# A two-layer hybrid encoder: the feed-forward features in other parts, more seven-product pairs in two units, and the first unit's copies dealt out

## The chip, the core and the metric

The kernel runs on one core of a Trainium2 chip. The core has TensorE (PE, the matmul engine; PEld is its weight load), VectorE (DVE), ScalarE (ACT), GpSimd (POOL) and SyncE (SP), which issues most of the transfers. The metric is the device time of one execution in microseconds (us). The kernel before takes 1952.31 us, the median of 3 runs (1952.17 to 1952.49).

## What is computed

One sequence of 256 tokens of width 2048 goes through two residual layers. Layer 0 mixes tokens by attention, layer 1 by a gated recurrence; behind each mixer stands a feed-forward block with 5632 features. All numbers are float32. The part that this change is about is the feed-forward block:

```python
def swiglu(h, w_gate, w_up, w_down):
    return (jax.nn.silu(h @ w_gate) * (h @ w_up)) @ w_down

for i in range(DEPTH):                      # DEPTH = 2
    h = rms_norm(x, norm_mix[i])
    mix = attention_mixer(...) if i % 2 == 0 else recurrent_mixer(...)
    x = x + mix
    x = x + swiglu(rms_norm(x, norm_ffn[i]), w_gate[i], w_up[i], w_down[i])
```

## The kernel before

**Number format.** To keep float32 precision, each operand is split into a rounded part `hi` and a rest `lo`. A product of two blocks of 128 x 128 by 128 x 512 is then three matmuls (`product`, lines 321 to 327): hi by hi, lo by hi, hi by lo. Weights arrive in `raw` tiles of 512 KB through SP's queue. ScalarE casts `raw` to `hi` (line 145, or 163 and 170), and VectorE takes the rest `lo = raw - hi` (line 146, or 164 and 171). Rings of buffers (`landing`, `parts`) let the loads, the casts and the rests run ahead of TensorE by a few tiles.

**Units.** The feed-forward features are worked on in eleven units of four tiles of 128 features (512 features). The units are numbered from 0. For one unit, the 2048 input features are read in eight chunks `c`; each chunk brings one tile of gate weights and one of up weights. There are two ways to multiply a chunk:

- *plain*: two loads (`load_half`), eight products, 24 matmuls. VectorE does two rests of 128 x 1024.
- *a seven-product pair* (`load_seven`, lines 154 to 195): the gate and up blocks are combined in the manner of Strassen so that seven products do, 21 matmuls. VectorE does two rests of 128 x 1024 (line 164), three combinations of 128 x 512 (line 169) and three rests of them (line 171); ScalarE casts accordingly (lines 163 and 170). One more sum, `t1`, is made by an accumulating transfer on POOL's queue (line 176), or by VectorE (line 174) where the three loads in front are all plain.

`SEVEN` names the chunks that are seven-product pairs: 0, 1, 2, 4, 5, 6. `FEWER` names another set for single units: unit 0 has three (0, 5, 6), unit 1 three (4, 5, 6), unit 2 four (1, 4, 5, 6). All other units have six.

**The end of a unit.** When a unit's products are done, VectorE and ScalarE put the four sums together (lines 769 to 773 and 791 to 795), apply SiLU and multiply. VectorE transposes the result in blocks of 32 (line 408), and sixteen small copies (line 416) bring the blocks to their places. A last cast and rest (lines 801 and 802) make the `hi` and `lo` of the features for the down product. With `beside` true, the sixteen copies are not done at once: they are put on the list `tail` in four lots of four, and each following `load_seven` takes one lot (lines 179 and 180), the fourth together with the last cast and rest. Before the change this is so for units 1 to 9; unit 0 and unit 10 do theirs at once, unit 0 with all sixteen on ScalarE.

**Parts.** The down product sums over features, and the sums are made part by part. `PARTS` counts the tiles of the parts: 8, 8, 8, 8 and 12, that is two units each and three in the last. `ffn_plan` (lines 208 to 215) writes out the order of the work. After each unit of part p + 1 come two of the four down groups (512 output columns each) of part p. A group of a part with 8 tiles is 48 matmuls in two accumulators. ScalarE evicts each accumulator to a tile `form` (line 818; two such tiles take turns) and POOL's queue adds it to the residual `x` by an accumulating transfer (line 821). The last part is handled by `groups` (lines 355 to 364): its last unit has just been computed, so two groups first do the tiles that were ready earlier (`front`), then the rest; each finished group is added to `x` by VectorE and, in layer 0, its norm is taken (`Norm.add`); in layer 1 it is stored.

**What sets the order.** TensorE's order is the order of the program. The casts and the rests follow one another in program order (`behind`); the rest of the order on the other engines is set by a scheduler with a timeline. `ahead` and `parted` hold small rules for it: `ahead` lets the n-th rest from now on come after a given instruction; `parted` holds evictions of odd down groups, which the next `load_seven` places behind its casts (lines 191 and 192). The argument `soon` of `unit` chooses earlier places for the end of a unit; it is true for the units of the first part.

Of the kernel before, what the change touches and what calls it, by code (L numbers as in the profile page):

```python
# [24 lines left out]
GROUP = NQ // NKV  # L25
NBLK = 8
DFF = 5632
PARTS = [8, 8, 8, 8, 12]
UNIT = 4
SEVEN = (0, 1, 2, 4, 5, 6)  # L30
FEWER = {0: (0, 5, 6), 1: (4, 5, 6), 2: (1, 4, 5, 6)}
HALF = 8
CHUNK = HALF * P
WIDE = 512
# [40 lines left out]
def trunk(ctx, tc, w, out):  # L75
    nc = tc.nc
    act, dve, pool, pe, sync = nc.scalar, nc.vector, nc.gpsimd, nc.tensor, nc.sync
# [11 lines left out]
    def nm(s):  # L89
        uid[0] += 1  # L90
        return f"{s}_{uid[0]}"

    def tmp(tag, shape=(P, S), dt=F32, bufs=2):
        pl = tp if tag in COMMON else scope[-1]
        return pl.tile(list(shape), dt, tag=tag, name=nm(tag), bufs=bufs)
# [4 lines left out]
    def follow(i, j):  # L100
        tc.add_manual_dep(
            i.ins, j.ins.name,
            mybir.DependencyInfo(mybir.DependencyClass.NoSync, mybir.DependencyReason.DATA),
            reason="order",
        )


    ring, held, ft, ahead, tail, parted = [0], [], [], [], [], []
# [95 lines left out]
    def out_order(src, late=1):  # L204
        groups = [pairs(src[g]) for g in range(NW)]
        return sum([g[:-late] for g in groups[:2]] + [g[-late:] for g in groups[:2]] + groups[2:], [])

    def ffn_plan():
        at = np.cumsum([0] + PARTS) // UNIT
        plan = [("unit", i) for i in range(at[1])]  # L210
        for p in range(len(PARTS) - 1):
            for n, i in enumerate(range(at[p + 1], at[p + 2])):
                plan.append(("unit", i))
                plan += [("down", (p, g)) for g in range(2 * n, min(2 * n + 2, NW))]
        return plan

    def ffn_order(l):
        seq = []
        for what, i in ffn_plan():
# [3 lines left out]
            both = [(w[f"w_gate{l}"][i, c], w[f"w_up{l}"][i, c]) for c in range(KT // 2)]  # L223
            seq += sum(([b] if c in (FEWER.get(i, SEVEN)) else list(b) for c, b in enumerate(both)), [])
        return seq + out_order(w[f"w_down{l}_{len(PARTS) - 1}"], UNIT // 2)

# [11 lines left out]
    def half():  # L238
        n = taken[0]
        taken[0] += 1  # L240
        if n == 0:
            return load_half(order[n], 2, first_x, 2)
        if n < KT // 2 and n % 2 == 0:
            load_x(2 * n, 4)
        if n == KT // 2 - 2:
            load_tables()
        got = load_seven(order[n], all(isinstance(o, bass.AP) for o in order[n - 3 : n])) if isinstance(order[n], tuple) else load_half(order[n], 2 if n == 1 else 1)
        g = n - KT // 2 - 1
        if 0 <= g < NW:
            sl = slice(g * WIDE, (g + 1) * WIDE)  # L250
            follow(sync.dma_start(out=x_tm[:, :, sl], in_=w["xt"][:, :, sl]), newest["load"])
        g -= 1
        if 0 < g <= NW:
            follow(newest["cast"], newest["square"])
        if 0 <= g < NW:
            token_squares(g)
        return got
# [22 lines left out]
    def new_acc():  # L280
        return ps_a.tile([P, 2 * S], F32, tag="acc", name=nm("acc"))
# [36 lines left out]
    def block(xs, k, a):  # L318
        return tuple(xs[k][:, s + a * P : s + (a + 1) * P] for s in (0, S))

    def product(o, x, wt, start, stop):
        (xh, xl), (wh, wl) = x, wt
        pe.matmul(o, xh, wh, start=start, stop=False)  # L323
        pe.matmul(o, xl, wh, start=False, stop=False)  # L324
        step()
        pe.matmul(o, xh, wl, start=False, stop=stop)  # L326
        step()

    def wide(accs, xs, k0, total, fresh=None):
        hi, lo = half()  # L330
        fresh = fresh or (k0 == 0, k0 == 0)
        for n in range(4):
            j, a = (n % 2, n // 2) if k0 + 2 == total else (n // 2, n % 2)
            part = [t[:, j * WIDE : (j + 1) * WIDE] for t in (hi, lo)]
            product(accs[a], block(xs, k0 + j, a), part, j == 0 and fresh[a], k0 + j == total - 1)
# [414 lines left out]
    def ffn(norm, nxt):  # L750
        def bank():
            return ps_m.tile([P, 2 * S], F32, tag="pm", name=nm("pm"))

        def unit(seven, beside, engines, soon):
            xs, r = norm.xs, [norm.r[:, a : a + 1] for a in range(2)]
            m1, p5, p6, p7 = (bank() for _ in range(4))
            c11, c21, c12, c22 = (new_acc() for _ in range(4))
            new = [m1, p5, p7, p6, c11, c21, c12, c22]

            def fresh(o):  # L760
                n = len(new)
                new[:] = [b for b in new if b is not o]
                return len(new) < n

            one, h = (tmp(n, (P, 2, WIDE), bufs=1) for n in ("one", "two"))
            (base, u), (v, x) = ([t[:, a, :] for a in range(2)] for t in (one, h))

            def sums():
                follow(act.copy(base, m1), newest["cast"])
                dve.tensor_tensor(u, base, p6, ALU.add)  # L770
                dve.tensor_tensor(v, u, p5, ALU.subtract)
                dve.tensor_tensor(u, u, p7, ALU.add)
                ahead.append([2, dve.tensor_tensor(x, u, p5, ALU.subtract), "rest"])

            for c in range(KT // 2):
                if c not in seven:
                    for pair in ((c11, c21), (c12, c22)):
                        wide(pair, xs, 2 * c, KT, [fresh(o) for o in pair])
                        if pair[0] is c11 and c == seven[-1] + 1:
                            sums()  # L780
                    continue
                wt, end = half(), c == seven[-1]
                n1, n3, n2, n4 = norm.forms[c]
                a11, a12, a22 = block(xs, 2 * c, 0), block(xs, 2 * c + 1, 0), block(xs, 2 * c + 1, 1)
                for o, y, b in (
                    (m1, a11, "b11"), (c11, a12, "b21"), (p5, n1, "t1"), (c12, n4, "b22"),
                    (p6, n2, "t2"), (p7, n3, "t3"), (c21, a22, "t4"),
                ):
                    product(o, y, wt[b], fresh(o), end and any(o is m for m in (m1, p5, p7, p6)))
            for o, y, b in ((base, base, c11), (u, u, c21)):  # L790
                features = dve.tensor_tensor(o, y, b, ALU.add)
            for a, (o, y, b) in enumerate(((base, v, c12), (u, x, c22))):
                table_act(o, o, AF.Silu, scale=r[a])
                last = dve.tensor_tensor(y, b, y, ALU.subtract)  # L794
            dve.tensor_tensor(h, h, one, ALU.mult)
            ahead.extend([[1 if soon else 3, features, "rest"], [2 if soon else 4, last, "rest"]])
            t, ht = act_four(), turn_blocks(h, engines, h, tail if beside else None)

            def whole(move=list):
                move()  # L800
                act.copy(t[:, :, :S], ht)
                dve.tensor_tensor(t[:, :, S:], ht, t[:, :, :S].bitcast(F32), ALU.subtract)

            if beside:
                tail.append(partial(whole, tail.pop()))
            else:
                whole()
            return [t[:, k, :] for k in range(UNIT)]

        hid = [[] for _ in PARTS]  # L810
        ends = np.cumsum(PARTS) // UNIT
        for what, i in ffn_plan():
            if what == "unit":
                hid[int(np.searchsorted(ends, i, "right"))] += unit(FEWER.get(i, SEVEN), 0 < i < ends[-1] - 1, (act,) if i < ends[-1] - 1 else (act, dve), i < ends[0])
            else:
                for a, acc in enumerate(wide_project(hid[i[0]], PARTS[i[0]], bank)):
                    t = tmp("form", (P, WIDE))
                    m = act.activation(t, acc, AF.Copy, scale=norm.r[:, a : a + 1])
                    if i[1] % 2:
                        parted.append(m)  # L820
                    pool.dma_start(out=x_tm[:, a, i[1] * WIDE : (i[1] + 1) * WIDE], in_=t, accum_op=ALU.add)
        if nxt is not None:
            ln_exp_tables()
        groups(hid[-1], PARTS[-1], PARTS[-1] - UNIT, lambda: None, partial(add_residual, norm=nxt, store=nxt is None, scale=norm.r))
        scope.pop()
        ft.pop().close()


    nr = Norm("norm_mix", KT)
    ffn(nf, nr)  # L830


# [210 lines left out]
```

## Time and profile before

| | |
|---|---|
| median of 3 runs | 1952.31 us |
| the profiled execution, its own time | 1952.89 us |
| its span in the trace | 1951.1 us |
| ScalarE, busiest group: casts of plain loads (line 145) | 474 times, 1045 ns each |
| VectorE, busiest group: rests of plain loads (line 146) | 474 times, 1240 ns each |
| rests of pairs (line 164) | 232 times, 1217 ns each |
| evictions (line 818) | 64 times, 689 ns each |
| moved by DMA | 426.42 MB, mean 219 GB/s |

The page of the profile gives busy times over the whole span. Where the limits change from stretch to stretch, the view of busy time by stretch is read beside it: it gives the length of each stretch and the busy time and count of instructions of each engine in it. A matmul's own duration in the trace is longer than its pitch, since matmuls are pipelined, so the time of a stretch is held against the number of matmuls in it. In the timelines, a row gives the start, the length and the engine, the line, the operation and its tiles, and in brackets how long the engine was idle in front of it and for whom. Where several instructions overlap, the row gives the time from the first start to the last end.

### The profile page before, as it was taken

The numbers are of one execution on the slowest core, as the hardware profiler recorded it, in microseconds if no ns is written. First come the engines' busy times: TensorE is split into PE (matmuls) and PEld (weight loads), VectorE is DVE, ScalarE is ACT, GpSimd is POOL, SyncE is SP. The second block draws the span as 40 slices with busy tenths as digits, with TensorE's granted clock in tenths as the row PEclk, the third lists the DMA queues.
The fourth block names the chain that finished last, engine by engine and source line by source line (L and its number), as shares of the span: only waits on it lengthen the run. The fifth ranks groups of instructions, "written<-read, shape, count | busy, mean of one in ns | idle before, by whom it ended". The sixth has DMA issues, their size and how long they took to land.

```text
span 1951.1 us, 27630 instructions
## 1 busy us (share of the span) xinstructions
PE 1938.0 (99%) x9224; PEld 1624.0 (83%) x9224; DVE 1768.6 (91%) x2417; ACT 1448.3 (74%) x2358; POOL 401.3 (21%) x497
## 2 busy tenths in 40 slices
PE   9999999999999999999999999999999999999999
PEld 8898888788888888888899998887888888888887
DVE  7878698999999999998799997898999999999993
ACT  7677686777777777777698887866778776787772
POOL 0442250011101111010465450520101111011100
PEclk9999999999999999999999999999999999999999
DMA  8434746698878978787365556555878888788872
GB/s 328 156 127 152 248 158 197 196 272 236 248 233 243 262 240 246 235 244 246 126 223 188 189 164 245 175 194 174 253 236 248 245 248 253 231 246 251 246 257 86
DMA packets 131727, 426.42 MB, mean 219 GB/s; under 512 B 14720, under 2 KB 14976, under 8 KB 131584
## 3 DMA queue, kind: packets, MB, share of 16 engines
q1 hardware_dynamic: 108944, 383.21, 58.0%
q0 software_dynamic: 22496, 41.43, 11.9%
q8 instruction: 72, 1.18, 0.2%
q14 instruction: 71, 0.58, 0.1%
q10 hardware_dynamic: 144, 0.02, 0.0%
HBM read 382.13 MB, written 2.10 MB: 197 GB/s over the span
## 4 chain that ended last, share of the span: by engine, by line
PE 92%; DVE 4%; ACT 1%; issue 1%; DMA 1%; POOL 0%; SPq 0%; ACTq 0%; DVEq 0%; POOLq 0%
PE acc L326 14%; PE acc L323 14%; PE acc L324 14%; PE pm L326 11%; PE pm L323 11%; PE pm L324 11%; PE acc L294 8%; PE acc L292 4%; PE pm L306 1%; PE pm L307 1%; PE pm L305 1%; DVE lo L146 1%; ACT hi L145 1%; DVE lo L164 0%; DMA raw<-in_w_in_dram 0%
## 5 line engine op out<-in xcount | busy, mean ns | idle before, releaser
L146 DVE TENSOR_TENSOR lo<-raw,hi 128x1024 fp32r<-128x1024 f32 (+1 forms) x474 | 574.5, 1240 | 77.1 <-ACT hi L145 75.3
L145 ACT CAST hi<-raw 128x1024 fp32r<-128x1024 f32 (+1 forms) x474 | 478.4, 1045 | 116.5 <-PE acc L324 72.1
L326 PE MATMUL acc<-lo,xg 128*128 128x512 f32 x744 | 290.9, 391 | 2.0 <-DVE lo L146 1.8
L323 PE MATMUL acc<-hi,xg 128*128 128x512 f32 x744 | 290.0, 390 | 0.0
L324 PE MATMUL acc<-hi,xg 128*128 128x512 f32 x744 | 289.6, 389 | 0.0
L164 DVE TENSOR_TENSOR lo<-raw,hi 128x1024 fp32r<-128x1024 f32 x232 | 275.0, 1217 | 6.5 <-ACT hi L163 3.8
L294 PE MATMUL acc<-xg,hi 128*128 128x512 f32 x832 | 271.7, 397 | 0.6 <-ACT hi L145 0.6
L163 ACT CAST hi<-raw 128x1024 fp32r<-128x1024 f32 x232 | 234.6, 1048 | 41.0 <-issue 14.4
L176 POOL DMA_DIRECT2D raw<-raw x90 | 77.7, 863 | 903.9 <-DVE raw L174 369.5
L323 PE MATMUL pm<-hi,act 128*128 128x512 f32 x512 | 199.2, 389 | 0.0
L324 PE MATMUL pm<-hi,act 128*128 128x512 f32 x512 | 199.2, 389 | 0.0
L326 PE MATMUL pm<-lo,act 128*128 128x512 f32 x512 | 199.2, 389 | 0.0
L416 ACT COPY two<-one 32x256 f32<-32x256 f32 x420 | 169.7, 404 | 24.7 <-DVE one L408 16.5
L292 PEld LDWEIGHTS acc<-xg,lo 128*128 128x128 f32 x832 | 156.3, 188 | 35.4 <-DVE lo L146 2.8
L323 PE MATMUL acc<-hi,act 128*128 128x512 f32 x448 | 174.9, 390 | 0.4 <-DVE two L794 0.4
L326 PE MATMUL acc<-lo,act 128*128 128x512 f32 x448 | 174.4, 389 | 0.0
L324 PE MATMUL acc<-hi,act 128*128 128x512 f32 x448 | 174.4, 389 | 0.0
L292 PE MATMUL acc<-xg,lo 128*128 128x256 f32 x832 | 171.8, 281 | 1.2 <-DVE lo L146 1.2
L326 PEld LDWEIGHTS acc<-lo,xg 128*128 128x128 f32 x744 | 139.7, 188 | 34.1 <-DVE lo L146 5.4
L324 PEld LDWEIGHTS acc<-hi,xg 128*128 128x128 f32 x744 | 139.7, 188 | 29.2
L323 PEld LDWEIGHTS acc<-hi,xg 128*128 128x128 f32 x744 | 139.7, 188 | 28.6
L170 ACT CAST hi<-raw 128x512 fp32r<-128x512 f32 x232 | 137.1, 622 | 32.8 <-DVE raw L169 31.8
(221 smaller groups left out, 3852.1 us busy)
## 6 DMA issues: line engine op xcount, KB each, us to landing
raw<-in_w_gate_dram SPq DMA_DIRECT2D x176, 512.0 KB, 4.6
raw<-in_w_up_dram SPq DMA_DIRECT2D x176, 512.0 KB, 5.5
raw<-in_w_down_dram SPq DMA_DIRECT2D x176, 512.0 KB, 4.4
raw<-in_w_in_dram SPq DMA_DIRECT2D x64, 512.0 KB, 4.4
raw<-raw POOLq DMA_DIRECT2D x90, 256.0 KB, 5.8
raw<-in_w_q_dram SPq DMA_DIRECT2D x32, 512.0 KB, 3.8
raw<-in_w_o_dram SPq DMA_DIRECT2D x32, 512.0 KB, 4.2
x<-form POOLq DMA_DIRECT2D x64, 256.0 KB, 6.7
```

The lines of the kernel that those rows point to most:

```text
L145: behind("cast", act.copy(hi[:, sl], raw[:, sl]))
L146: behind("rest", dve.tensor_tensor(lo[:, sl], raw[:, sl], hi[:, sl].bitcast(F32), ALU.subtract))
L163: behind("cast", act.copy(hi, src))
L164: behind("rest", dve.tensor_tensor(lo, src, hi[:].bitcast(F32), ALU.subtract))
L170: behind("cast", act.copy(hi, o))
L176: pool.dma_start(out=t1, in_=b11, accum_op=ALU.add)
L292: pe.matmul(acc[:, S:], w, xs[k][:, :S], start=False, stop=stop)
L294: pe.matmul(acc, w, xs[k], start=(k == 0), stop=stop)
L323: pe.matmul(o, xh, wh, start=start, stop=False)
L324: pe.matmul(o, xl, wh, start=False, stop=False)
L326: pe.matmul(o, xh, wl, start=False, stop=stop)
L416: m = (eng.copy if eng is act else eng.tensor_copy)(to[:, :, :, i, :], of[:, :, :, j, :])
```

## The change

```diff
-PARTS = [8, 8, 8, 8, 12]
+PARTS = [4, 8, 8, 8, 8, 8]
 UNIT = 4
 SEVEN = (0, 1, 2, 4, 5, 6)
-FEWER = {0: (0, 5, 6), 1: (4, 5, 6), 2: (1, 4, 5, 6)}
+FEWER = {0: (0, 5, 6), 1: (1, 2, 4, 5, 6), 2: (0, 1, 4, 5, 6)}
...
             if what == "unit":
-                hid[int(np.searchsorted(ends, i, "right"))] += unit(FEWER.get(i, SEVEN), 0 < i < ends[-1] - 1, (act,) if i < ends[-1] - 1 else (act, dve), i < ends[0])
+                hid[int(np.searchsorted(ends, i, "right"))] += unit(FEWER.get(i, SEVEN), i < ends[-1] - 1, (act,) if i < ends[-1] - 1 else (act, dve), i < ends[0])
...
                     pool.dma_start(out=x_tm[:, a, i[1] * WIDE : (i[1] + 1) * WIDE], in_=t, accum_op=ALU.add)
+        parted.clear()
```

- The first part has one unit, and the five others two each. The order becomes unit 0; unit 1 and two down groups of part 0; unit 2 and the other two; unit 3 and two groups of part 1; and so on to unit 10, which is followed by the last two groups of part 4. A group of part 0 has 24 matmuls. The last part has 8 tiles instead of 12, so its last two groups have 48 matmuls instead of 72, and its `front` groups have 24 each instead of 48. There are five parts with evictions and accumulating transfers instead of four: 40 of each per layer instead of 32.
- Units 1 and 2 have five seven-product pairs each, instead of three and four.
- Unit 0's copies go to `tail` and are dealt out to the `load_seven`s of unit 1.
- `soon` is now true for unit 0 alone, since it is the only unit of the first part.
- `parted` is emptied at the end of the layer, because the last odd group now comes after the last `load_seven`.

## The prediction

> **What bounds the kernel now.** I read the page first. The span is 1951.1 us, the profiled execution took 1952.89 us, and the median of the runs shown is 1952.31 us; the difference from span to time (1.8 us) is left alone, and a change of the span is added to the median.
>
> ```profile
> span 1951.1 us, 27630 instructions
> PE 1938.0 (99%) x9224; PEld 1624.0 (83%) x9224; DVE 1768.6 (91%) x2417; ACT 1448.3 (74%) x2358; POOL 401.3 (21%) x497
> PE 92%; DVE 4%; ACT 1%; issue 1%; DMA 1%; POOL 0%; SPq 0%; ACTq 0%; DVEq 0%; POOLq 0%
> ```
>
> TensorE is busy 99% and carries 92% of the chain that ended last. Its busy time overlaps itself, so I look for the pitch of its matmuls instead. The reader must know which stretch is which: a product is three matmuls of 512 columns, a seven-product pair is 21 of them, a plain pair 24, and the order on TensorE is written out by the kernel. Counting from the first matmul of the feed-forward layer gives the borders. I number units from 0. The view of busy time by stretch (columns: stretch, length, busy us and count of PE, PEld, DVE, ACT, POOL, clock, DMA share, GB/s) shows unit 0, unit 1, unit 2 and unit 3 of layer 0, the first two wide groups of the last part, and then unit 1, unit 2 and those groups of layer 1:
>
> ```profile
> 266.39:307.87 41.48, 41.48 (x185) 34.35 (x183) 40.37 (x61) 33.10 (x54) 14.31 (x17) 1.00 0.57 182
> 307.87:349.75 41.88, 41.88 (x185) 34.19 (x183) 37.38 (x46) 27.32 (x43) 1.73 (x2) 1.00 0.64 210
> 349.75:394.44 44.69, 42.53 (x182) 33.33 (x181) 43.12 (x53) 33.39 (x50) 1.71 (x2) 1.00 0.63 202
> 416.19:455.63 39.44, 39.44 (x175) 32.67 (x174) 38.49 (x50) 32.13 (x46) 4.33 (x5) 1.00 0.76 230
> 884.03:906.34 22.31, 22.10 (x97) 17.94 (x96) 21.68 (x27) 14.66 (x20) 0.00 (x0) 1.00 0.89 302
> 1304.86:1346.75 41.89, 41.87 (x185) 34.20 (x183) 37.19 (x45) 26.69 (x41) 1.74 (x2) 1.00 0.65 212
> 1346.75:1391.43 44.68, 42.49 (x182) 33.31 (x180) 43.05 (x53) 33.30 (x50) 1.71 (x2) 1.00 0.62 201
> 1881.03:1903.29 22.26, 22.05 (x97) 17.94 (x96) 21.67 (x27) 13.36 (x19) 0.00 (x0) 1.00 0.89 304
> ```
>
> Unit 0 is 3 x 21 + 5 x 24 = 183 matmuls in 41.48 us: 0.2267 us each. Unit 3 (6 x 21 + 2 x 24 = 174) takes 39.44 us, again 0.2267. So TensorE runs at its pitch there, at a clock of 1.00. Unit 1 has 183 matmuls too and takes 41.88 us: 0.40 lost. Unit 2 has 180, worth 40.80 us, and takes 44.69: 3.89 lost. Layer 1 loses 0.41 and 3.88. The first two groups of the last part (96 matmuls, 21.76 us) lose 0.55 and 0.50. That is nearly all that TensorE loses in the two feed-forward layers: 2 x 4.29 + 1.05 = 9.6 us.
>
> **Who makes it lose.** In the timeline of ScalarE and VectorE I look for the first thing that is late before unit 2:
>
> ```profile
> 320.76 6.64 ACT L416 COPY two<-one 32x256 f32<-32x256 f32 x16 [1.11 <-DVE one L408]
> 328.08 0.69 DVE L171 TENSOR_TENSOR olo<-raw,ohi 128x512 fp32r<-128x512 f32 x1 [4.19 <-ACT ohi L170]
> ```
>
> Unit 0's sixteen copies stand on ScalarE in one block of 6.64 us, casts queue behind them, and VectorE sits idle for 4.19 us for the cast `ohi`. Apart from this, VectorE is nearly full in these stretches: 43.12 of 44.69 us in unit 2, and 38.49 of 39.44 in unit 3. So the lost 4.29 us per layer come from VectorE falling behind by 4.19. TensorE waits for VectorE's rests `lo`, and VectorE has no room to catch up.
>
> How much VectorE costs per pair decides the rest. Its timeline in unit 3 (one seven-product pair, from one L164 to the next) and in unit 2 (four rests of plain loads in a row):
>
> ```profile
> 435.47 2.36 DVE L164 TENSOR_TENSOR lo<-raw,hi 128x1024 fp32r<-128x1024 f32 x2
> 437.86 0.69 DVE L169 TENSOR_TENSOR raw<-raw 128x512 f32<-128x512 f32 x1
> 438.59 1.29 DVE L169 TENSOR_TENSOR raw<-raw,raw 128x512 f32<-128x512 f32 x2
> 439.80 0.69 DVE L171 TENSOR_TENSOR olo<-raw,ohi 128x512 fp32r<-128x512 f32 x1
> 440.40 1.29 DVE L171 TENSOR_TENSOR lo<-raw,hi 128x512 fp32r<-128x512 f32 x2
> 441.61 2.35 DVE L164 TENSOR_TENSOR lo<-raw,hi 128x1024 fp32r<-128x1024 f32 x2
> ...
> 362.39 4.63 DVE L146 TENSOR_TENSOR lo<-raw,hi 128x1024 fp32r<-128x1024 f32 x4
> 366.94 0.68 DVE L174 TENSOR_TENSOR raw<-raw,raw 128x512 f32<-128x512 f32 x1
> ```
>
> A seven-product pair occupies VectorE for 441.61 - 435.47 = 6.14 us, while TensorE spends 21 x 0.2267 = 4.76 us on it: VectorE loses 1.38 us of lead. A plain pair costs VectorE 2 x (366.94 - 362.39) / 4 = 2.28 us against 24 x 0.2267 = 5.44 on TensorE: it wins 3.16.
>
> **The change part by part.** *Five sevens in units 1 and 2* (the title's units 2 and 3). Unit 1 goes from three to five, unit 2 from four to five: three pairs per layer, six in all. TensorE loses 3 matmuls per pair: 18 x 0.2267 = 4.08 us in all, 2.04 per layer. VectorE gains 6.14 - 2.28 = 3.86 us per pair, 11.6 us per layer. ScalarE gets three half casts more per pair; it is busy 33.39 of 44.69 us in unit 2, so that work is hidden by its idle time. Each new pair that follows a pair also sends one add through POOL's queue, which is busy under 2 us in units 1 and 2.
>
> The Trainium skill's page "TensorE: Matmul & The Clock Gate" (section "Back-to-back issue gap") gives about 131 ns per matmul of 512 columns as the sustained rate; by that estimate the 18 matmuls would be worth 2.36 us. No stretch here runs so fast: 183 matmuls in 41.48 us decide.
>
> *Unit 0's copies dealt out.* They go in fours to the first four sevens of unit 1, which now has five, so none is left over. The block of 6.64 us is gone and with it up to 4.19 us of VectorE's idle time per layer. What is late next is VectorE itself.
>
> *Parts of 4, 8, 8, 8, 8, 8.* The number of products with the down weights stays. Four groups of 24 matmuls now follow units 1 and 2 (two each), and the groups of 48 start after unit 3 instead of after unit 2. Behind the last unit, two groups of 48 matmuls now precede the groups of the last part, on other accumulator banks. The 0.55 and 0.50 us there should go: -1.05 us. On SP's queue the loads are as many and as large as before, and those of the first down weights come earlier by one unit. Each layer has eight evictions on ScalarE and eight accumulating DMAs on POOL's queue more; they are priced below.
>
> *The sum goes by VectorE.* I take a point that both versions reach with the same work behind them: units 0 to 3 and 96 matmuls of down products. Before, it is the third down group at 455.63 us; after, the first down group of the second part. VectorE's rests for it, and for the start of unit 1, stand here:
>
> ```profile
> 306.24 1.22 DVE L146 TENSOR_TENSOR lo<-raw,hi 128x1024 fp32r<-128x1024 f32 x1
> 453.68 2.35 DVE L146 TENSOR_TENSOR lo<-raw,hi 128x1024 fp32r<-128x1024 f32 x2
> ```
>
> Unit 1's first rest is done at 307.46 us and needed at 307.87: VectorE's lead is only 0.41 us when the change begins to bite. At the common point the first rest ends 453.68 + 1.22 = 454.9 us, 0.7 us ahead. After the change VectorE gets there 11.6 us later for the new work and 4.2 us earlier for the idle time that goes: 462.3 us. TensorE can begin a product two matmuls (0.45 us) before its rest is done, so it starts at 461.9 to 462.3, which is 6.2 to 6.6 us after 455.63. I take 6.4 per layer. The 2.04 us of matmuls are not subtracted again, because VectorE sets the time. From there the cycle is that of unit 3 onwards, which ran without loss. Less about 0.5 at the last part: 5.9 per layer, 11.8 us for two.
>
> How much of VectorE's idle time may go is bounded by its waits between 266 and 456 us (us in total, times, longest):
>
> ```profile
> DVE olo L171 <- ACT ohi L170: 4.6, 2, 4.2
> DVE one L770 <- ACT one L769: 0.8, 1, 0.8
> DVE lo L164 <- ACT hi L163: 0.6, 1, 0.6
> ```
>
> If all 6.0 us went, not 4.2, a layer would be 1.8 us cheaper: 8.2 us for both. That is the low end.
>
> *Evictions of the short groups.* Two tiles `form` take turns. One pair of evictions, their DMAs and the landing times of such DMAs:
>
> ```profile
> 526.55 0.69 ACT L818 ACTIVATE form<-pm,nr 128x512 f32<-128x512 f32 x1 [3.21 <-PE pm L326]
> 527.54 0.86 POOL L821 DMA_DIRECT2D x<-form  x1
> 530.33 1.21 POOL L821 DMA_DIRECT2D x<-form  x1
> DMA to landing us min/median/max: 3.4/7.2/8.3
> L171 DVE TENSOR_TENSOR olo<-raw,ohi 128x512 fp32r<-128x512 f32 x6 | 4.1, 685 | 0.9 <-ACT ohi L170 0.9
> ```
>
> A group of 24 matmuls lasts 5.44 us, so the next eviction would be due at 526.55 + 5.44 = 532.0, while the tile comes free at 527.54 + 7.2 = 534.7, and the other one at 537.5 instead of 533.4. An eviction that waits holds all that is queued behind it on ScalarE: casts, and so VectorE's rests and TensorE. The Trainium skill's page "TensorE: Matmul & The Clock Gate" (table at its top, row on queue depth) calls ScalarE's queue a strict FIFO; by that, the casts behind the eviction could not pass, and the upper price below would hold. Bounds: nothing, if the eviction is queued behind casts that VectorE still lives on, up to 4.1 us at each of two places per layer. The nearest row is VectorE's 0.9 us per unit for a cast behind evictions; I take 0.9 once per layer: 1.8 us. A gain below nothing is excluded, as no eviction is removed.
>
> *End of layer 0.* The last two groups shrink from 72 to 48 matmuls, 10.88 us instead of 16.32, and the next norm's squares, copies and scales must fit between:
>
> ```profile
> 917.22:933.54 16.32, 16.32 (x73) 13.52 (x72) 10.38 (x14) 13.68 (x27) 6.33 (x14) 1.00 0.30 100
> 933.54:950.00 16.46, 16.46 (x74) 13.65 (x73) 9.78 (x12) 11.97 (x24) 3.16 (x8) 1.00 0.38 124
> ```
>
> ScalarE has 13.68 and 11.97 us of work here, two casts fewer in each after (about 2 us): 11.7 and 10.0 in 10.88. It fits on the mean, and may overrun by about 1 to 4 us once. I take nothing, since ScalarE is ahead by casts at that point; 4 us goes to the high end.
>
> Sum: 11.8 + 1.8 = +13.6 us, 1952.3 + 13.6 = **1965.9 us** (1966.5 for the profiled execution).
>
> **The rivals.** (a) *The copies were the whole trouble* and VectorE keeps up. Then 4.08 + 8.58 + 1.05 = 13.7 us go: 1938.6 us. For it speaks that the 4.19 us of idle time and the 4.29 lost are almost one number. Against it: VectorE would have to reach the common point 1 us earlier than before, with 11.6 us more work, and the windows of units 0 to 3 above hold only 1.1 + 4.5 + 1.6 + 1.0 = 8.1 us in which it is idle. TensorE comes out even where VectorE arrives at most 1.7 us later (its lead of 0.7, the 0.45 and the 0.5 of the last part), so the point from which this decides is a new pair that costs VectorE (4.2 + 1.7) / 3 = 2.0 us instead of 3.86. (b) *VectorE's idle time goes altogether*, all 8.1 us per layer instead of 4.2, and no eviction waits: 11.8 - 2 x 3.9 = +4.0 us, 1956.3, and a little less if the new pairs come cheaper. (c) *The evictions bind*: four places at 4.1 us: 11.8 + 16.4 = +28 us, 1980.5. (d) *The copies aren't dealt out in fact*: dealt to pairs whose casts already follow closely, they hold VectorE up as before, and the 4.2 us per layer stay: 11.8 + 8.4 + 1.8 = +22 us, 1974.3.
>
> **How the numbers follow.** Forecast 0.72; (a) 0.07; (b) 0.10; (c) 0.06; (d) 0.05. A measurement of this kernel can tell about 0.2%, 3.9 us, from no change. The forecast, (c), (d) and a little of (b) are slower by more: 0.85. The rest of (b) is within: 0.08. (a) is faster: 0.07. The range runs from +2.7 us, which takes in the low end of 8.2 and most of (b), to +24.7 us, which takes in (d), the layer's end and half of (c): 1955 to 1977.
>
> **What would show it.** Right: TensorE at 0.2267 us from unit 4 on, losses of about 13 us per layer up to the common point (6.4 + 2.04 + 4.29; now 4.29), unit 3 losing for the first time, VectorE over 97% busy from unit 1 to unit 3, no 16 copies in a row before unit 1's sevens, no loss in the first groups of the last part. Wrong: unit 3 still at 39.44 us, or VectorE idle for over 5 us between unit 0 and the common point, or a seven-product pair under 4.3 us on VectorE.

## The result and the profile after

The changed kernel takes 1978.42 us (median of 4 runs, 1977.85 to 1979.38) beside 1952.24 us for the kernel before on the same chip: a ratio of 1.0134, 95% interval 1.0117 to 1.0152. It is slower, as forecast, but by 26 us instead of 13.6, outside the range. The profiled execution took 1977.85 us, the least of the four. The page after, with the lines that answer to those shown of before:

```profile
span 1976.0 us, 27715 instructions
PE 1950.8 (99%) x9206; PEld 1619.1 (82%) x9206; DVE 1794.2 (91%) x2453; ACT 1467.5 (74%) x2392; POOL 418.9 (21%) x519
PE 81%; DVE 10%; issue 3%; ACT 3%; DMA 2%; POOL 1%; SPq 0%; DVEq 0%; ACTq 0%; POOLq 0%
```

TensorE has 18 matmuls less, and yet its share of the chain that ended last falls from 92% to 81%; VectorE's rises from 4% to 10%. The busy time by stretch in layer 0 (unit 0, unit 1, unit 2, unit 3, and the `front` groups of the last part):

```profile
266.51:307.99 41.48, 41.48 (x184) 34.35 (x183) 40.36 (x61) 31.01 (x52) 15.19 (x18) 1.00 0.60 188
307.99:353.89 45.90, 43.31 (x179) 32.37 (x178) 45.00 (x57) 34.27 (x52) 2.56 (x3) 1.00 0.65 198
364.79:408.05 43.26, 41.92 (x179) 32.69 (x178) 40.63 (x52) 36.24 (x55) 3.47 (x4) 1.00 0.75 222
418.93:465.44 46.51, 43.48 (x175) 31.56 (x174) 43.49 (x57) 37.97 (x58) 4.30 (x5) 1.00 0.79 219
915.62:926.50 10.88, 10.88 (x49) 9.01 (x48) 5.65 (x5) 4.80 (x6) 1.72 (x2) 1.00 0.97 273
```

Units 1 and 2 now have 177 matmuls, worth 40.12 us at 0.2267; unit 3 still has 174, worth 39.44. They lose 5.8, 3.1 and 7.1 us: 16.0 in layer 0, and by the same reckoning 16.0 in layer 1, where before it was 4.8 in each. The `front` groups lose nothing (48 matmuls, 10.88 us). Unit 3, whose own pairs the change leaves as they were, loses most. The first down group after it starts at 465.44 us; before, the same work was behind TensorE at 455.63. That is the common point of the prediction.

The sum: losses 16.02 + 16.04 - 4.82 - 4.78 = +22.5 us, matmuls -4.1, and one more place, the end of layer 0. From the last matmul of layer 0's feed-forward block to the first of layer 1's, TensorE needs 319.97 us (959.15 to 1279.12) instead of 313.52 (949.86 to 1263.38): +6.45. Together +24.8, against 24.9 us between the spans.

VectorE's waits between 266 and 466 us (us in total, times, longest), as those shown of before:

```profile
DVE lo L164 <- ACT hi L163: 3.6, 3, 2.0
DVE olo L171 <- ACT ohi L170: 1.4, 3, 0.5
DVE one L770 <- ACT one L769: 0.8, 1, 0.8
DVE act L802 <- ACT act L801: 0.2, 1, 0.2
```

The wait of 4.2 us behind the block of copies is gone, but the sum is 6.0 us, where the same view of before has 6.4 (the three rows shown and two of 0.2 us). In layer 1 it rises, from 7.9 to 8.9 us. Most of the new waiting is for `hi` of line 163. In the timeline this stands in front of the second pair of units 2 and 3, behind ScalarE's evictions:

```profile
367.71 1.26 ACT L818 ACTIVATE form<-pm,nr 128x512 f32<-128x512 f32 x2
...
421.85 0.68 ACT L818 ACTIVATE form<-pm,nr 128x512 f32<-128x512 f32 x1
423.19 0.69 ACT L818 ACTIVATE form<-pm,nr 128x512 f32<-128x512 f32 x1 [0.66 <-DMA x<-form]
```
```profile
369.94 2.36 DVE L164 TENSOR_TENSOR lo<-raw,hi 128x1024 fp32r<-128x1024 f32 x2 [1.24 <-ACT hi L163]
424.85 2.36 DVE L164 TENSOR_TENSOR lo<-raw,hi 128x1024 fp32r<-128x1024 f32 x2 [2.01 <-ACT hi L163]
```

In unit 3 the second eviction, at 423.19, waits 0.66 us until the transfer from its `form` tile has landed; in unit 2 neither waits. The casts of the next pair stand behind both, so most of the 1.24 and 2.01 us is the evictions' own time on ScalarE.

At the end of layer 0, POOL's half of the copies that turn the groups for the next norm shows when each group's turn came, after and before:

```profile
935.52 4.35 POOL L416 COPY two<-one 32x256 f32<-32x256 f32 x8 [17.13 <-DVE one L408]
947.38 4.32 POOL L416 COPY two<-one 32x256 f32<-32x256 f32 x8 [7.51 <-DVE xg L436]
959.26 3.45 POOL L416 COPY two<-one 32x256 f32<-32x256 f32 x8 [7.56 <-DVE xg L436]
967.80 1.76 POOL L416 COPY two<-one 32x256 f32<-32x256 f32 x4 [5.09 <-DVE xg L436]
```
```profile
927.22 4.32 POOL L416 COPY two<-one 32x256 f32<-32x256 f32 x8 [7.48 <-DVE xg L436]
939.20 3.45 POOL L416 COPY two<-one 32x256 f32<-32x256 f32 x8 [7.67 <-DVE xg L436]
953.76 1.74 POOL L416 COPY two<-one 32x256 f32<-32x256 f32 x4 [11.12 <-DVE nm L480]
```

After the change the second and the third group each come 11.9 us behind the one in front; before, the third came 12.0 us behind the second. The next group may only be turned when the scale `xg` of the one before has read the pair of buffers `one` and `two`. (The last group, whose copies VectorE shares, follows 8.5 us after the third.) Before, the last group waited for its own norm sum (11.12 us of idle time for `nm`) and came 3.9 us after its matmuls ended at 949.86. After, groups end 10.88 us apart, it waits for the buffers, and comes 8.6 us after 959.15. TensorE then waits twice for `xg`, and the granted clock (the share of TensorE's full clock in the windows view, the last figure but two) falls to one half behind the second wait:

```profile
966.54 0.50 PE L294 MATMUL acc<-xg,hi 128*128 128x512 f32 x1 [1.66 <-DVE xg L436]
971.80 0.80 PE L294 MATMUL acc<-xg,hi 128*128 128x512 f32 x1 [2.12 <-DVE xg L436]
```
```profile
971.60:978.40 6.80, 6.46 (x20) 5.33 (x21) 6.55 (x11) 5.24 (x9) 2.92 (x9) 0.50 0.44 127
```

The theory to be tried has three parts. **V**: VectorE's total work sets the time up to the end of unit 3. **G**: evictions on ScalarE delay casts there. **N**: the single pair of turning buffers sets the end of layer 0.

### The profile page after: what moved, and what is told of

Its sections match the earlier page's. It is cut to its first block, busy times and chain, and to the rows that moved or that the text cites. A ratio compares the mean times of both kernels' runs of the same rounds, so it can differ in the third digit from the quotient of the medians.

```text
span 1976.0 us, 27715 instructions
## 1 busy us (share of the span) xinstructions
PE 1950.8 (99%) x9206; PEld 1619.1 (82%) x9206; DVE 1794.2 (91%) x2453; ACT 1467.5 (74%) x2392; POOL 418.9 (21%) x519
## 4 chain that ended last, share of the span: by engine, by line
PE 81%; DVE 10%; issue 3%; ACT 3%; DMA 2%; POOL 1%; SPq 0%; DVEq 0%; ACTq 0%; POOLq 0%
PE acc L326 11%; PE acc L323 11%; PE acc L324 11%; PE pm L326 10%; PE pm L324 10%; PE pm L323 10%; PE acc L294 8%; PE acc L292 4%; DVE lo L164 2%; DVE raw L169 2%; DVE lo L146 1%; PE pm L306 1%; PE pm L307 1%; PE pm L305 1%; ACT two L416 1%
## 5 line engine op out<-in xcount | busy, mean ns | idle before, releaser
L145 ACT CAST hi<-raw 128x1024 fp32r<-128x1024 f32 (+1 forms) x462 | 465.9, 1045 | 105.0 <-PE acc L324 65.0
L164 DVE TENSOR_TENSOR lo<-raw,hi 128x1024 fp32r<-128x1024 f32 x244 | 289.8, 1219 | 9.3 <-ACT hi L163 7.5
L326 PE MATMUL acc<-lo,xg 128*128 128x512 f32 x708 | 277.5, 392 | 0.1
L323 PE MATMUL acc<-hi,xg 128*128 128x512 f32 x708 | 276.2, 390 | 0.0
L324 PE MATMUL acc<-hi,xg 128*128 128x512 f32 x708 | 275.7, 389 | 0.0
L326 PE MATMUL pm<-lo,act 128*128 128x512 f32 x576 | 224.1, 389 | 0.0
L324 PE MATMUL pm<-hi,act 128*128 128x512 f32 x576 | 224.1, 389 | 0.0
L323 PE MATMUL pm<-hi,act 128*128 128x512 f32 x576 | 224.1, 389 | 0.0
L169 DVE TENSOR_TENSOR raw<-raw,raw 128x512 f32<-128x512 f32 x244 | 158.7, 690 | 3.5
L171 DVE TENSOR_TENSOR lo<-raw,hi 128x512 fp32r<-128x512 f32 x244 | 158.5, 690 | 0.0
L324 PEld LDWEIGHTS acc<-hi,xg 128*128 128x128 f32 x708 | 132.9, 188 | 27.9
L170 ACT CAST ohi<-raw 128x512 fp32r<-128x512 f32 x122 | 75.6, 620 | 106.4 <-DVE raw L169 106.2
L323 PEld LDWEIGHTS acc<-hi,xg 128*128 128x128 f32 x708 | 133.0, 188 | 26.4
```

The costliest lines, as they stand in the source:

```text
L145: behind("cast", act.copy(hi[:, sl], raw[:, sl]))
L164: behind("rest", dve.tensor_tensor(lo, src, hi[:].bitcast(F32), ALU.subtract))
L169: behind("rest", dve.tensor_tensor(o, x, y, op))
L170: behind("cast", act.copy(hi, o))
```

## The experiments

Two edits return below: *lots*, which deals unit 0's copies in three lots where unit 1 has only three pairs, and *second buffers*.

```diff
 # lots (with "i < ends[-1] - 1" for "0 < i < ends[-1] - 1" in the call of unit)
+                if i == 0:
+                    tail[:2] = [partial(lambda a, b: (a(), b()), *tail[:2])]
 # second buffers (in Norm.turn; more is used in turn_blocks in place of one and two)
+            more = None
+            if self.g == ("norm_mix", KT) and g % 2:
+                more = act_four()[:].bitcast(F32)
```

The table has, for each kernel, the median, the ratio to the kernel before with its 95% interval, what TensorE loses in the feed-forward block of layer 0 (its length less 0.2267 us per matmul), and how much longer than before (313.52 us) it is from the end of that block to layer 1's. The last two come from the trace of one execution. The kernel before was measured beside each set of runs, at 1952.24 to 1953.05 us, and the ratio goes by that; a difference of medians between rows of two sets can be off by the 0.8 us between these.

| kernel | us | ratio | lost in layer 0's block | to layer 1's, against before |
|---|---|---|---|---|
| before | 1952.24 | | 4.8 | 0 |
| after | 1978.42 | 1.0134 (1.0117 to 1.0152) | 16.0 | +6.5 |
| copies alone | 1950.87 | 0.9989 (0.9979 to 0.9998) | 4.1 | -0.3 |
| pairs alone | 1977.79 | 1.0126 (1.0110 to 1.0143) | 19.9 | -1.2 |
| parts alone | 1963.93 | 1.0055 (1.0040 to 1.0070) | 6.8 | +6.4 |
| pairs and copies | 1967.76 | 1.0075 (1.0060 to 1.0090) | 15.3 | -1.2 |
| parts and pairs | 1986.56 | 1.0170 (1.0156 to 1.0184) | 20.4 | +5.5 |
| parts and copies | 1959.92 | 1.0038 (1.0023 to 1.0052) | 5.9 | +4.5 |
| after, second buffers | 1971.98 | 1.0097 (1.0082 to 1.0112) | 16.2 | -0.3 |
| after, evictions free | 1989.33 | 1.0188 (1.0173 to 1.0203) | 21.5 | +6.0 |
| after, five pairs in unit 3 | 1972.14 | 1.0096 (1.0079 to 1.0113) | 11.6 | +8.3 |
| copies, pair later | 1950.88 | 0.9984 (0.9976 to 0.9993) | 2.2 | +4.1 |
| best, four pairs in unit 3 | 1946.51 | 0.9967 (0.9955 to 0.9980) | 0.0 | +0.7 |
| best, five pairs in unit 3 | 1953.19 | 1.0001 (0.9992 to 1.0010) | 1.8 | +4.7 |

**Copies alone.** The kernel before with *lots*.

> The kernel before with unit 0's copies dealt out and nothing else (three lots, since unit 1 has only three seven-product pairs). Theory V (VectorE sets the time in units 0 to 3, and the block of copies costs it 4.2 us per layer): VectorE's idle 4.19 us goes, and with it most of the 4.29 us that TensorE loses per layer: 6 to 8.5 us less, 1944 to 1946 us. Rival E (the copies cost what they cost wherever they stand; the loss only moves): 1952 us, the same.

1950.87 us: 2 us less instead of 6 to 8.5, so rival E is nearer than V. My reading of the profile before fell here. Of the idle 4.19 us 0.87 remain, but VectorE, now ahead, meets other waits before the sums at the end of unit 1, one for ScalarE and one for TensorE; the busy time of unit 2 follows:

```profile
343.62 0.69 DVE L770 TENSOR_TENSOR one<-one,pm 128x512 f32<-128x512 f32 x1 [0.89 <-ACT one L769]
345.68 0.69 DVE L791 TENSOR_TENSOR one<-one,acc 128x512 f32<-128x512 f32 x1 [0.65 <-PE acc L326]
```
```profile
349.56:393.91 44.35, 42.56 (x182) 33.31 (x180) 42.35 (x52) 32.61 (x49) 1.71 (x2) 1.00 0.63 200
```

Unit 2 (180 matmuls, 40.80 us) still loses 3.55 us. My reading is that VectorE's lead can't be carried over the end of a unit that no down groups follow: the sums of unit 1 wait, and rests of unit 2 stand behind them. That 4.19 us of idle time and 4.29 lost are nearly equal says nothing of a cause: with 3.3 us of that wait gone, TensorE loses 0.7 us less in layer 0.

**Copies, pair later.** The same, with unit 2's first pair moved back by one chunk.

```diff
-FEWER = {0: (0, 5, 6), 1: (4, 5, 6), 2: (1, 4, 5, 6)}
+FEWER = {0: (0, 5, 6), 1: (4, 5, 6), 2: (2, 4, 5, 6)}
```

> The kernel before with the copies dealt out, and unit 2's first pair at chunk 2 instead of chunk 1. Theory B (with the copies dealt out what is left in unit 2 is that VectorE must finish unit 1, whose end stands right in front of it without down groups between, so that a pair two chunks later finds VectorE free): the 1.9 and 0.4 us behind the start of chunk 1 go, 1945 to 1948 us. Rival (VectorE's total work decides, the place of the pair does not): 1950 to 1951 us, as with the copies alone.

A median of 1950.88 us, as the rival said, but not for its reason: the trace shows theory B's gain, 2.2 us lost instead of 4.1 in layer 0, and 2.2 instead of 3.5 in layer 1. In this execution it is given back outside, between the two blocks (+4.1 us), where TensorE waits once in the recurrent mixer and the clock halves behind that wait:

```profile
1005.36 0.47 PE L294 MATMUL acc<-xg,hi 128*128 128x512 f32 x1 [2.14 <-DVE act L381]
```
```profile
1006.40:1009.70 3.30, 3.30 (x13) 2.91 (x12) 3.23 (x7) 3.20 (x8) 1.11 (x4) 0.50 0.54 158
```

The median hides two groups: six of the eleven runs took 1950.9 to 1951.4 us at a mean granted clock of 0.999, this one among them, and five took 1948.7 to 1949.2 us at 1.000. The five are about 1.7 us under the copies alone, so theory B's gain shows in them, though short of the 1945 to 1948 us that it expected.

**Pairs alone.** The new `FEWER` in the kernel before.

> The kernel before with five seven-product pairs in units 1 and 2 and nothing else. Theory V: 11.6 us more VectorE work per layer where VectorE has about 1 us of lead to give at the common point, so about 10 us per layer more: 1970 to 1975 us. Rival S (the parts are what made it slower; the pairs save 18 matmuls): 1948 us.

1977.79 us, 3 us over the top of the range of V and far from the rival. The 18 matmuls saved are worth nothing here. The block of copies now stands in unit 1's first pair, where VectorE waits 5.42 us for `ohi`. TensorE then waits for up to 6.2 us at a time, and the granted clock is at one half for 23.9 us in all inside units 1 and 2 of both layers. What the half clock adds is not separated by any run; unit 2 loses 8.7 us with 6.8 us of it (layer 0) and 8.3 us with 3.4 (layer 1), so it seems little.

**Parts alone.** The new `PARTS`, with `parted.clear()`.

> The kernel before with the new parts and nothing else (unit 0's copies in one block, three and four pairs in units 1 and 2). Theory V with two additions read from the profile after: the layer's end 6.5 us, once; the evictions of the short groups hold ScalarE and so VectorE 1.2 to 2 us at two places per layer; the first groups of the last part gain 1.05: 1952.2 + 6.5 + 6 - 1 = 1963 to 1964 us. Rival (only the new pairs cost anything): 1951 us.

1963.93 us, as expected: units 1 and 2 lose 0.4 us instead of 4.3, unit 3 loses 6.4 instead of nothing, and the layer's end is 6.4 us longer. So unit 3 loses with the new parts alone, without any new pair: before it there are now 48 matmuls of down groups instead of 96.

**Pairs and copies.** The new `FEWER` and unit 0's four lots, with the old parts.

> The kernel before with the five pairs and the dealt-out copies, and the old parts. Theory V: per layer 11.6 us more work less 4.2 us of idle time and about 1 us of lead, 6 to 7 us: 1964 to 1967 us. If instead the new parts carry the cost: 1940 to 1948 us.

1967.76 us, a little over the range of V; the rival is out. Dealing out is worth 10 us here and 2 us alone. With the old parts VectorE's waits in layer 0 do fall, from 6.4 to 4.0 us.

**Parts and pairs.** The change without the dealt-out copies.

> The change without the dealt-out copies: new parts and five pairs in units 1 and 2, unit 0's sixteen copies in one block. Theory V: VectorE has no lead to give in unit 1, so the block costs its whole idle time of about 4 to 5 us per layer, as it does between the two kernels with old parts and five pairs (10 us together): 1986 to 1989 us. Rival (the block costs about 2 to 4 us together, as with three and four pairs): 1980 to 1982 us.

1986.56 us, as V expected. With no lead, the block costs its whole idle time: unit 1 loses 10.6 us instead of 5.8, and VectorE's wait is 5.42 us instead of 0.46:

```profile
314.70 6.61 ACT L416 COPY two<-one 32x256 f32<-32x256 f32 x16 [3.46 <-DVE one L408]
```
```profile
321.98 0.69 DVE L171 TENSOR_TENSOR olo<-raw,ohi 128x512 fp32r<-128x512 f32 x1 [5.42 <-ACT ohi L170]
```

So of the three edits only the copies help, by 7 to 8 us in this company.

**Parts and copies.** The new parts with *lots* and the old `FEWER`.

> The kernel before with the new parts and the dealt-out copies (three lots), with three and four pairs in units 1 and 2. From the parts alone 1963.9 us: theory V says that the 4.2 us of VectorE's idle time behind the block of copies is now worth its length, since short down groups stand behind unit 1 and VectorE can keep its lead into unit 3: 3 to 4 us per layer less, 1956 to 1958 us. Rival (as in the run with the copies alone, which gained 1 to 2 us): 1961 to 1963 us.

1959.92 us, between the two ranges: 4 us under the parts alone. By the traces 0.9 and 1.1 us of the gain lie in the two blocks and 1.9 between them. V expected more: units 1 and 2 lose nothing now, but unit 3 still loses 5.9. As in the run with the copies alone, the lead won does not reach unit 3.

**After, five pairs in unit 3.**

```diff
-FEWER = {0: (0, 5, 6), 1: (1, 2, 4, 5, 6), 2: (0, 1, 4, 5, 6)}
+FEWER = {0: (0, 5, 6), 1: (1, 2, 4, 5, 6), 2: (0, 1, 4, 5, 6), 3: (1, 2, 4, 5, 6)}
```

> The changed kernel with five seven-product pairs instead of six in unit 3, that is 3 matmuls more per layer (0.68 us) and 3.86 us less VectorE work. Theory V (VectorE sets the time up to the end of unit 3): 3 to 4 us per layer less, 1970 to 1972 us, though TensorE has more to do. Rival M (the matmul count sets the time): 1.4 us more, 1979.8 us.

1972.14 us: 6.3 us less with 6 matmuls more. Unit 3 loses 2.5 us instead of 7.1 in layer 0 and 3.0 instead of 6.5 in layer 1. M is out; between the two this decides for V.

**After, second buffers.**

> The changed kernel, in which the turning of every second group at the end of layer 0 uses a free feature tile instead of the one pair of buffers (one, two). Theory N (the 6.4 us at the end of layer 0 come from the four groups standing in line for one pair of buffers, some 12 us each, where the groups now last 10.9 us instead of 16.3): most of it goes, 1972 to 1974 us, and the half clock near 972 us in the trace goes too. Rival A (ScalarE has too much work there): no change, 1978 us.

1971.98 us: 6.4 us less, as N said; the layer's end is as short as before (-0.3). The turns of the first two groups now follow closely, and the clock stays at 1.00 there:

```profile
935.84 4.35 POOL L419 COPY two<-one 32x256 f32<-32x256 f32 x8 [17.13 <-DVE one L411]
940.25 4.35 POOL L419 COPY act<-act 32x256 f32<-32x256 f32 x8
```
```profile
959.50:972.00 12.50, 12.20 (x70) 10.20 (x69) 12.02 (x28) 10.88 (x24) 4.94 (x13) 1.00 0.26 78
```

**After, evictions free.** Without the rule for odd down groups.

```diff
-                    if i[1] % 2:
-                        parted.append(m)
```

> The changed kernel without the rule that places the evictions of odd down groups behind the casts of the next pair. Theory G (VectorE's idle 1.2 and 2.0 us in front of the second pair of units 2 and 3 is ScalarE working on those evictions, late because the tiles form are still in use): it goes or is smaller, 2 to 3 us per layer, 1972 to 1975 us. Rival: ScalarE waits for the tiles at another place and holds the casts there: 1978 us or more.

1989.33 us, 11 us more. As a remedy it failed: the scheduler now puts the evictions in front of the first pair's casts, in line 170, where ScalarE waits for TensorE and VectorE for ScalarE:

```profile
365.90 0.69 ACT L818 ACTIVATE form<-pm,nr 128x512 f32<-128x512 f32 x1 [4.92 <-PE acc L324]
```
```profile
370.08 0.69 DVE L171 TENSOR_TENSOR olo<-raw,ohi 128x512 fp32r<-128x512 f32 x1 [3.94 <-ACT ohi L170]
```

It shows the mechanism of G (an eviction that isn't ready holds the casts behind it), with a larger price; TensorE's waits of up to 3.8 us there halve the clock three times inside units 2 and 3, so that the 11 us are not the eviction's alone. That removing the evictions' delay in the changed kernel would give back the 3.3 us of layer 0 was not shown by any run.

**Best, four and five pairs in unit 3.** New parts, *lots*, *second buffers*, the old three and four pairs in units 1 and 2.

```diff
-FEWER = {0: (0, 5, 6), 1: (4, 5, 6), 2: (1, 4, 5, 6)}
+FEWER = {0: (0, 5, 6), 1: (4, 5, 6), 2: (1, 4, 5, 6), 3: (1, 4, 5, 6)}  # five: 3: (1, 2, 4, 5, 6)
```

> A version for speed: new parts, dealt-out copies (three lots), the second pair of turning buffers, three and four pairs in units 1 and 2, and four pairs instead of six in unit 3. Theory V: from 1959.9 us (parts and copies) the layer's end gives 4 to 5 us, unit 3's loss of 5.8 us per layer goes for 1.36 us of matmuls: 1945 to 1947 us, under the kernel before. If VectorE's lead is lost elsewhere instead: 1950 us or more.

> The same with five pairs in unit 3. Theory V: 3.9 us less VectorE work per layer against a loss of 5.8, 0.68 us of matmuls: about 1 to 2 us per layer stay lost, 1947 to 1949 us, a little more than with four pairs. Rival (the matmul count decides between the two): 1.4 us less than with four.

With four pairs 1946.51 us, as V expected: faster than both kernels. Units 1, 2 and 3 of layer 0 run at the pitch (183, 180 and 180 matmuls):

```profile
307.70:349.18 41.48, 41.48 (x185) 34.35 (x184) 38.69 (x46) 30.11 (x46) 1.73 (x2) 1.00 0.67 215
360.06:400.86 40.80, 40.80 (x182) 33.78 (x181) 36.92 (x46) 34.14 (x51) 3.43 (x4) 1.00 0.76 230
411.74:452.54 40.80, 40.80 (x182) 33.78 (x181) 36.91 (x46) 33.94 (x51) 3.47 (x4) 1.00 0.77 232
```

VectorE's waits for casts are no shorter here (us in total, times, longest, 266 to 470 us), but it has the room to make up for them:

```profile
DVE lo L146 <- ACT hi L145: 3.2, 2, 2.0
DVE lo L164 <- ACT hi L163: 2.1, 2, 1.4
DVE olo L171 <- ACT ohi L170: 1.8, 3, 0.9
```

With five pairs it is 1953.19 us, not 1947 to 1949. The 1.8 and 1.5 us lost in unit 3 were expected; the 4.7 us at the end of layer 0 were not. There TensorE waits 2.5 us once, where it waits 1.5 with four pairs, and the clock is at half for 3.4 us; why that wait differs between the two kernels I leave open. Between the two traced executions lie 5.6 us: 3.9 at the end of layer 0 and only 2.0 in the two blocks, which is about what V expected there.

## Why the prediction was wrong

- *Direction and place were right, the engine in part.* TensorE runs at 0.2267 us per matmul outside units 1 to 3 (but for 0.33 us in unit 4 of layer 1), unit 3 loses for the first time, and the `front` groups gain the 1.05 us. A seven-product pair still takes 6.14 us of VectorE in the changed kernel (319.53 to 325.67 us), and one pair less in unit 3 makes the kernel faster. But one of the prediction's own signs of being wrong came true: between unit 0 and the common point VectorE is idle for 6.6 us (0.9, 2.6 and 3.0 in units 1 to 3), not under 5, and it is busy for 94% of units 2 and 3, not for over 97%.
- *The step that failed first*: "11.6 us later for the new work and 4.2 us earlier for the idle time that goes". The work came, but the idle time did not go: from the start of unit 0 to the common point all of VectorE's idle time is 7.7 us after and 8.2 before. New waits took the place of the old: 3.3 us behind the evictions, 1.4 us behind the lots of copies, where I had "0.9 once per layer". The rest was ready 465.66 us into the span instead of 462.3. TensorE reached the common point 9.8 us later instead of 7.3 (6.4 and 0.9). That is 2.4 us per layer with the start of the block 0.1 us later, 4.8 in all.
- *The step that failed second*: "I take nothing, since ScalarE is ahead by casts at that point". ScalarE's busy time was the wrong thing to add up. The pair of buffers sets the pace, 11.9 us per group, which no busy share shows; the run with second buffers gives back 6.4 us. 13.6 + 4.8 + 6.4 = 24.8 us, the difference of the spans.
- *By edit, the miss is in the parts.* My terms for the pairs and the copies add up to 12.8 us, and the run with these two measured +14.9. My terms for the parts (two evictions at 0.9, less 1.05, and nothing for the layer's end) add up to 0.8 us, and the run with the parts alone measured +11.0. The two sums make 25.9 us, nearly the 26.2 of the whole change. By the trace of the parts alone 6.4 us of its cost lie at the end of layer 0 and 3.9 in the two blocks.
- *"So the lost 4.29 us per layer come from VectorE falling behind by 4.19"* was wrong too: the copies alone bring 2 us, not 8.
- *The rivals*: (a), the copies as the whole trouble, is refuted by the run with the copies alone. My argument against it had a slip: without losses the common point would come 6.3 us sooner, and VectorE would have to be there about 5 us earlier than before, not 1. (b) is refuted by the waits. (c) had the right engine at two fifths of its price (1.2 and 2.0 us at the two places, not 4.1), and only 0.66 us of that is an eviction that waits for its tile. (d) did not happen: the lots are in the trace, and VectorE waits 1.4 us behind them, not 4.2. That the true time was the sum of a part of (c) and the layer's end, each kept for the high end alone, is why the range was too low.

## What to carry to other kernels

Where an engine feeds another just in time, count its work and its lead up to a point that both versions reach with the same work done; the matmuls saved are worth nothing before that while the other engine sets the time. Don't subtract an idle time that an edit removes unless the engine's next wait has been looked for: here nearly all of it came back behind other instructions of ScalarE's queue. And for a stage that gets shorter, look not only for busy shares but for the buffer that its steps hand on: its cycle time (here 11.9 us) is a bound that shows only in the spacing of starts.

## What the runs showed of the hardware

The granted clock fell to one half behind waits of TensorE, for 3.4 or 6.8 us at a time: in the changed kernel behind a wait of 2.12 us (6.8 us at half clock), and for 3.4 us each behind 2.14 us (copies with the pair later), 2.49 us (best with five pairs) and 1.89 us (parts and copies). The length of a single wait does not decide: with the evictions free a wait of 2.64 us was followed by no fall, and neither was one of 2.12 us in the kernel with five pairs in unit 3.

```profile
958.60 0.50 PE L294 MATMUL acc<-xg,hi 128*128 128x512 f32 x1 [1.89 <-DVE xg L436]
```
```profile
370.11 0.51 PE L323 MATMUL pm<-ohi,fh 128*128 128x512 f32 x1 [2.64 <-ACT ohi L170]
```

Where the wait lies in time does matter. Within one execution the falls lie on a grid of 3.41 us: with the pairs alone they come at 320.81, 365.18, 1327.74 and 1375.53 us, 13, 282 and 14 steps apart. If the time without a matmul is added up in each step of that grid, the step in front of every fall, but for the one at the program's end, held 1.76 us or more. Steps at full clock with 1.66 us or less were followed by none; of those between 1.76 and 1.93 us three were and two were not. The wait of 2.64 us was split between two steps, 1.10 and 1.53 us. The Trainium skill's page "TensorE: Matmul & The Clock Gate" (Part 1, "What's actually happening") says that the clock is halved after an idle window of about 3.4 us; the lengths at half clock agree with one and two such windows. In these traces a wait clearly shorter than the window was enough. If a microsecond at half clock does the work of half a microsecond, 6.8 us of it cost up to 3.4 us beside the wait itself where TensorE sets the pace; that is an estimate.
